# A two-model kernel: modulation sums off the tensor engine, one more early expert load, keys among the last transposes, outputs turned once per bank

## The chip, the cores and the metric

The kernel runs on one core of one Trainium2 chip. The metric is the device time of one execution in microseconds, as a median over runs; less is better. Everything is 32-bit floating point. A product in plain fp32 shows in the trace as two matmul entries; where three products of rounded parts take its place (`mm3`), each entry is one product of the fp32r type.

## What is computed

Two transformer blocks follow each other on the same 512 tokens of width 1024. Cut to what matters:

```python
# first block
m_lat = jnp.split((s_lat @ w_mod[l] + b_mod[l])[:, None, :], 6, axis=-1)
h_lat = modulate(rmsnorm(x_lat, norm1_g[l]), m_lat[0], m_lat[1])
mix_lat, mix_ctx = token_mixers(h_lat, h_ctx, w_in[l], ...)
x_lat = x_lat + m_lat[2] * (mix_lat @ w_out[l])
h_lat = modulate(rmsnorm(x_lat, norm2_g[l]), m_lat[3], m_lat[4])
x_lat = x_lat + m_lat[5] * expert_choice_ffn(h_lat, w_router[l], w_gate[l], w_up[l], w_down[l])
# second block
sh1, sc1, gt1, sh2, sc2, gt2 = jnp.split((jax.nn.silu(c) @ w_mod + b_mod)[:, None, :], 6, axis=-1)
x = x + gt1 * token_mixer(modulate_2(x, g, sh1, sc1), ...)
x = x + gt2 * conv_ffn(modulate_2(x, norm2_g[l], sh2, sc2), ...)
```

The six modulation vectors of a block are one 1024-vector times a 1024 by 6144 matrix. The experts are 16 gated networks of 24 MB each in all; each takes its 64 best tokens.

## The kernel before

The work is emitted by Python generators that are woven by weights (`weave`, `beside`); a scheduler then fixes each engine's order ahead of the run from these priorities and a model of times. On the chip every engine runs its own list in order, and a transfer is issued by the queue of the engine it stands on, nearly always SP's.

**Projections** (`g_proj`, L701 to 857, 52 to 222 us of the trace). Eleven blocks of 256 columns of `w_in` are loaded, split into a rounded part and a rest (`wsplit`, L1948 on: a copy on ScalarE, a subtraction on VectorE or GpSimd) and multiplied with the normed input. Results go through four PSUM banks. The block of values is written out from L789 on; convolution buffers `cr` and `cr2` are freed at the end.

**Modulation vectors** (`g_mods`, L652 on). Two half vectors of 512 columns make one vector. `mod_rows` (L510) loads a half vector's weights in four pieces of 512 KB into a ring of three buffers and multiplies eight k-steps, four of them in four column strips of the array; the two models' inputs stand as 32 weight columns. The row is copied out and then turned into the layout that is wanted: by transposes (`mod_cols`, L521), by products with the identity into a layout of 8 channels a partition (`mod_cols_pk`, L533), or spread over all partitions (`mod_bcast`, L545). Ten vectors are made this way beside the Fourier and the neighbourhood attention (`others`, L1464), while the delta rule (`g_dn`) is woven through.

**Experts** (`g_b`, L1617). Each expert has twelve loads of 2 MB: gate and up alternately, then down. They go into a ring of five buffers, later eight; `more` (L1633) lends rooms that are not used yet: expert 0's third load goes to the sum's room, its seventh to the inputs' room. The pair of experts gets its rows by an indirect transfer (`pair`, L1596) into `Y`, the same room that later takes the pair's output; the rows are transposed and scaled. The second model's context work (`g_c0`) is woven between and frees its room at its end; three more buffers then join the ring. `c_tile` (L2035) adds expert results to a tile of tokens, norms it, and at the last tile turns all four tiles in two halves (`to_hT2`, L1974) and splits them.

**Second mixer** (`part_c`). `c_att` begins with keys of two tiles at a time (`tok2`, L2004) and their rotation. `c_ssd` mixes values: for each pair of heads and each of four tiles of tokens, `mixed` (L2434) multiplies the weighted values, and adds the part `of` of the outer state by a product with the identity; both go to the same PSUM bank, which is scaled when its four tiles are done.

Of the kernel before, what the change touches and what calls it, by code (L numbers as in the profile page):

```python
# [390 lines left out]
class KA:  # L391
# [141 lines left out]
    def mod_cols_pk(self, s, wdram, bi, j, ring, rows, out):  # L533
        nc = self.nc
        t = self.big().rearrange("p (k g r) -> p k g r", k=8, g=4)
        for h in range(2):
            r = rows()
            self.mod_rows(s, wdram, 2 * j + h, ring, r)
            for kt in range(8):
                self.mm(t[64 * h:64 * h + 64, kt].rearrange("p g r -> p (g r)"), r[:, kt::8], self.ident)  # L540
        nc.vector.tensor_reduce(out, t[:, :, :, 0:2].rearrange("p c g r -> p c r g"), AX.X, OP.add)
        nc.vector.tensor_add(out, out, self.col("b_mod_pk", 8 * bi, 8)[:, :, None].to_broadcast([128, 8, 2]))
# [109 lines left out]
    def g_mods(self, tag, n):  # L652
        nc, I = self.nc, self.I
        self.md = tag
        with self.pool("mods") as P:
# [3 lines left out]
            self.mod_bcast(s1, wm, I["b_mod"], 2, wr, rows, self.gt1_b.ap(), self.sel)  # L659
            yield 0.1  # L660
            self.mod_cols_pk(s1, wm, 0, 3, wr, rows, mp[:, 0])
            yield 0.1
            self.mod_cols_pk(s1, wm, 1, 4, wr, rows, mp[:, 1])
            nc.vector.scalar_tensor_tensor(a2, mp[:, 1, :, 0], 1.0, self.col("norm2_g_pk", 0, 8), op0=OP.add, op1=OP.mult)
            yield 0.1
            self.mod_bcast(s1, wm, I["b_mod"], 5, wr, rows, self.gt2_b.ap(), self.sel)
            yield 0.1
            mc, a = self.m2c_b.ap(), self.ab2_b.ap()
            s2, wm = self.s2b.ap(), "w_mod_2"
            for i, j in enumerate((0, 1, 3, 4)):  # L670
                self.mod_cols(s2, wm, "b_mod_2", j, wr, rows, mc[:, i])
                yield 0.1
            for i, (m, r, n) in enumerate(((1, 0, "norm1_g_2"), (1, 1, "norm1_g_2"), (3, 0, "norm2_g_2"))):
                nc.vector.scalar_tensor_tensor(a[:, i], mc[:, m, :, r], 1.0, self.col(n, 0, 8), op0=OP.add, op1=OP.mult)
            for i, j in enumerate((2, 5)):
                for h in range(2):
                    r, g = rows(), rows()[0:1]
                    self.mod_rows(s2, wm, 2 * j + h, wr, r)
                    t = self.bank((128, 512), self.md)
                    self.mm(t, self.sel, r)  # L680
                    self.ld(g, I["b_mod_2"][0:1, 512 * (2 * j + h):512 * (2 * j + h) + 512], nc.scalar)
                    nc.vector.tensor_add(g, g, t[0:1])
                    nc.scalar.dma_start(self.gtd[i:i + 1, 512 * h:512 * h + 512], g)
                yield 0.1
# [16 lines left out]
    def g_proj(self, P):  # L701
# [91 lines left out]
        for t in range(4):  # L793
            z = nv()
            self.cp(z, self.tok(w, t))
            if t == 0:
                left()
            nc.scalar.dma_start(vdv[:, t], z)
        yield 0.04
        for t in range(2):  # L800
            self.cp(vc[:, t], self.tok(w, t, False))
        w.done()
# [4 lines left out]
        for i in range(2):  # L807
            nc.scalar.mul(q[:, i].rearrange("p (i r c) -> p r i c", i=4, r=8), self.chan(w, 128 * i).rearrange("p (r i c) -> p r i c", i=4, r=8), 0.125)
            yield 0.03
        w.done()  # L810
        w = block()
        for i in range(2):
            self.cp(k[:, i], self.chan(w, 128 * i), "v")
            if i == 0:
                next(gates)
                self.abT_b.free()
            self.cp(kc[:, i], self.chan(w, 128 * i, False))
            yield 0.05
# [6 lines left out]
        for a in range(2):  # L825
            w = block()
            for t in range(4):
# [4 lines left out]
                for e in range(2):  # L832
# [3 lines left out]
                    (nc.gpsimd.tensor_sub if e == 0 else nc.gpsimd.tensor_add)(o[:, :, :, e], o[:, :, :, e], u)  # L836
                yield 0.015
            if a == 1:
                for t in range(2):
                    self.cp(kc[:, t].rearrange("p m d -> p (m d)"), self.tok(w, t, False))  # L840
                yield 0.03
            w.done()
        w = block()
        for t in range(2):
            self.cp(v[:, t], self.tok(w, t, False))
        yield 0.03
        for t in range(4):
            self.cp(v[:, 2 + t], self.tok(w, t))
        yield 0.06
        w.done()  # L850
        w = block()
        for i in range(2):
            self.cp(self.uT_b.ap()[:, i], self.chan(w, 128 * i))
            yield 0.03
        w.done()
        cr.free()
        cr2.free()
# [648 lines left out]
class KB(KA):  # L1506
# [89 lines left out]
    def pair(self, pr, Y):  # L1596
        nc = self.nc
# [3 lines left out]
        nc.gpsimd.indirect_dma_start(Y, None, self.xnd, bass.IndirectOffsetOnAxis(self.ix[:, pr:pr + 1], 0))  # L1601
        yield
        for k4 in range(2):
            b = self.bank((128, 4, 128))
            for kk in range(4):
                nc.tensor.transpose(b[:, kk], Y[:, 4 * k4 + kk::8], self.ident)
# [10 lines left out]
    def g_b(self, experts=range(16)):  # L1617
# [15 lines left out]
        more = [None, None, sum_b.ap(), None, None, None, in_b.ap()]  # L1633
# [120 lines left out]
class Kern(KB):  # L1754
# [219 lines left out]
    def to_hT2(self, xs, half, a, b, tmp, bank=None):  # L1974
# [3 lines left out]
        for k in range(0, 8, n):  # L1978
# [5 lines left out]
            for kk in range(n):  # L1984
# [5 lines left out]
                (nc.gpsimd if kt % 2 else nc.vector).tensor_sub(lo, u, hi.bitcast(F32))  # L1990

# [12 lines left out]
    def tok2(self, w, t0, nt, tag="mm"):  # L2004
        n = w(0, 0).shape[1]
        b = self.bank((128, nt, n), tag)
# [28 lines left out]
    def c_tile(self, t, b):  # L2035
# [14 lines left out]
        c["r"].append(z(3))  # L2050
        if t == 3:
            mc, a = self.m2c_b.ap(), self.ab2_b.ap()
            for i in range(2):
                self.to_hT2([c["xn"][:, 2 * i], c["xn"][:, 2 * i + 1]], i, a[:, 0], mc[:, 0, :, 0], c["u"], lambda: self.bank((128, 2, 256)))
# [12 lines left out]
    def c_att(self, P):  # L2067
# [32 lines left out]
        for half in range(2):  # L2100
            for t in range(0, 4, 2):
                b = self.tok2(w, t, 2)
# [169 lines left out]
    def c_ssd(self, P):  # L2272
# [84 lines left out]
        for gr in range(4):  # L2357
# [76 lines left out]
            def mixed(k):  # L2434
                pr, c = k // 4, k % 4
                if c == 0:
                    ys[pr] = self.bank((128, 512), "y")
                yb, W, tk = ys[pr], Ws.pop(k), slice(128 * c, 128 * c + 128)
                for z in range(2):
                    for h in range(2):  # L2440
                        o = 128 * pr + 64 * h
                        self.mm(yb[64 * h:64 * h + 64, tk], (of if z else xs)[:, c, o:o + 64], self.ident if z else W[:, h], z == 0, z == 1)
# [338 lines left out]
```

## Time and profile before

| what | us |
|---|---|
| median of 3 runs (2982.39 to 2989.98) | 2982.91 |
| the profiled execution | 2982.76 |
| its span | 2980.9 |
| TensorE busy in the span | 2770.4 |
| VectorE | 1334.9 |
| ScalarE | 902.3 |
| GpSimd | 625.7 |

The span is what the profiler sees between the first and the last instruction; the rest of the profiled execution's time lies around it. A busy TensorE is one with matmuls in flight. Loading of weights is counted apart, since it runs beside the matmuls. The shares are means over stretches with different limits, so the rows below are taken by stretch. "Idle before" names what an engine waited for last.

### The profile page before, as it was taken

To read this page: it belongs to the slowest core of one execution; us is meant where nothing else is said; L and a number is where in the kernel's file an instruction comes from. 1 tells how busy PE (TensorE), PEld (TensorE's weight loads), DVE (VectorE), ACT (ScalarE), POOL (GpSimd) and SP (SyncE) were. 2 spreads that over 40 slices of the span, in tenths; PEclk is the share of its full clock that TensorE was granted. 3 is DMA by queue.
4 is the path that set the end of the run, shared out by engine and by line. 5 is a ranking of instruction groups with operands and counts; after the bars stand their busy time and mean duration, and the time that the engine had idled before them with its cause. 6 is when DMAs were issued, how large, how long until landed. Compare 5 with 4: busy or idle time off the path is not lost.

```text
span 2980.9 us, 41808 instructions
## 1 busy us (share of the span) xinstructions
PE 2770.4 (93%) x16824; PEld 1776.0 (60%) x16824; DVE 1334.9 (45%) x2654; ACT 902.3 (30%) x1836; POOL 625.7 (21%) x660
## 2 busy tenths in 40 slices
PE   7999989997999999988888789999999899999998
PEld 4894547765334333332222267777777688888886
DVE  5522445655121211111101167878787854454445
ACT  5511225532111010100000044545454543343333
POOL 3121224531000000000000024232323322332222
PEclk9999999998999999999999999999999999999999
DMA  6216661038999999989999923324242464242331
GB/s 268 75 34 200 209 218 32 30 121 309 397 430 430 429 429 430 429 371 430 431 431 430 387 88 105 118 64 123 72 120 74 134 232 160 94 154 95 97 99 57
DMA packets 213122, 658.53 MB, mean 221 GB/s; under 512 B 13816, under 2 KB 131192, under 8 KB 188352
## 3 DMA queue, kind: packets, MB, share of 16 engines
q1 hardware_dynamic: 185504, 601.73, 52.4%
q10 hardware_dynamic: 26272, 49.93, 4.7%
q0 software_dynamic: 1152, 4.19, 0.3%
q8 instruction: 133, 2.18, 0.3%
q14 instruction: 61, 0.50, 0.1%
HBM read 632.07 MB, written 23.73 MB: 220 GB/s over the span
## 4 chain that ended last, share of the span: by engine, by line
PE 68%; DMA 16%; DVE 10%; issue 2%; ACT 2%; POOL 2%; SPq 1%; ACTq 0%; POOLq 0%; DVEq 0%
PE bank_mm L399 29%; PE bigbank L399 20%; DMA l<-in_w_up 6%; PE bank_pj L399 6%; DMA l<-in_w_down 4%; PE bank_c L399 4%; PE bank_dn L399 2%; DMA mods<-in_cola 2%; DMA l<-in_w_gate 1%; PE bank_sm L399 1%; DVE base L2426 1%; DVE mix L2430 1%; PE bank_dnr L399 1%; DVE mix L2429 1%; PE bank_mm L2181 1%
## 5 line engine op out<-in xcount | busy, mean ns | idle before, releaser
L399 PE MATMUL bank_pj<-c,c 128*128 128x512 f32 (+2 forms) x1368 | 319.7, 376 | 0.3 <-DVE c L1964 0.3
L399 PE MATMUL bank_mm<-c,c 128*128 128x512 f32 (+1 forms) x1608 | 304.4, 347 | 4.9 <-ACT b L1987 3.2
L399 PEld LDWEIGHTS bank_mm<-c,c 128*128 128x128 f32 x1608 | 259.3, 191 | 44.2 <-ACT b L1987 3.6
L399 PE MATMUL bigbank<-l 128*64 128x512 f32 (+1 forms) x1104 | 266.1, 594 | 17.9 <-DMA l<-in_w_up 13.1
L399 PEld LDWEIGHTS bank_pj<-c,c 128*128 128x128 f32 (+1 forms) x1368 | 225.7, 189 | 50.7 <-issue 17.5
L1963 ACT CAST c<-base 128x1024 fp32r<-128x1024 f32 x147 | 152.8, 1045 | 254.3 <-PE bigbank L399 105.7
L1964 POOL TENSOR_TENSOR c<-base,c 128x1024 fp32r<-128x1024 f32 x47 | 116.7, 2483 | 472.9 <-ACT c L1963 404.6
L1964 DVE TENSOR_TENSOR c<-base,c 128x1024 fp32r<-128x1024 f32 x100 | 136.3, 1365 | 136.8 <-ACT c L1963 133.7
L399 PEld LDWEIGHTS bigbank<-l 128*64 128x64 f32 (+1 forms) x1104 | 80.9, 141 | 175.8 <-issue 140.4
L1692 DVE TENSOR_TENSOR b<-l,bigbank 128x512 f32<-128x512 f32 x32 | 20.5, 683 | 340.8 <-PE bigbank L399 293.5
L1691 ACT ACTIVATE l<-bigbank 128x512 f32<-128x512 f32 x32 | 17.4, 595 | 423.7 <-PE bigbank L399 423.7
L399 PE MATMUL bank_mm<-l 128*64 128x512 f32 (+2 forms) x528 | 124.8, 601 | 9.1 <-DMA l<-in_w_down 8.0
L399 PE MATMUL bigbank<-out,c 128*128 128x512 f32 x480 | 113.8, 397 | 1.9 <-ACT out L2524 1.8
L399 PE MATMUL bank_c<-b 128*128 128x256 f32 (+3 forms) x496 | 110.0, 373 | 1.9 <-ACT b L425 0.8
L399 PE MATMUL bank_mm<-h,sp 128*128 128x512 f32 (+3 forms) x544 | 105.5, 382 | 4.3 <-ACT h L644 3.8
L399 PEld LDWEIGHTS bank_dn<-dn 64*64 64x64 f32 x1920 | 74.8, 134 | 55.0 <-issue 39.3
L399 PEld LDWEIGHTS bigbank<-out,c 128*128 128x128 f32 x480 | 91.7, 192 | 23.0 <-ACT out L2524 2.2
L399 PE MATMUL bigbank<-b,l 128*64 128x512 f32 x352 | 84.9, 614 | 21.8 <-DMA b<-in_w_up 10.9
L1717 DVE TENSOR_TENSOR b<-bank_mm,ab 64x512 f32<-64x512 f32 x16 | 10.9, 683 | 208.1 <-PE bank_mm L399 208.1
L1786 ACT ACTIVATE b<-bank_c,base 128x256 f32<-128x256 f32 x20 | 11.3, 563 | 304.6 <-PE bank_c L399 304.6
L399 PEld LDWEIGHTS bank_c<-b 128*128 128x128 f32 (+1 forms) x496 | 80.4, 188 | 37.2 <-issue 23.9
L399 PE MATMUL bigbank<-c,ffn 128*128 128x512 f32 x432 | 100.3, 390 | 0.0
(538 smaller groups left out, 5060.7 us busy)
## 6 DMA issues: line engine op xcount, KB each, us to landing
l<-in_w_up SPq DMA_DIRECT2D x36, 2048.0 KB, 14.6
l<-in_w_down SPq DMA_DIRECT2D x31, 2048.0 KB, 17.0
l<-in_w_gate SPq DMA_DIRECT2D x29, 2048.0 KB, 18.2
mods<-in_cola SPq DMA_DIRECT2D x80, 512.0 KB, 4.9
base<-in_w_in SPq DMA_DIRECT2D x68, 512.0 KB, 3.7
b<-in_w_gate SPq DMA_DIRECT2D x15, 2048.0 KB, 34.0
base<-in_w_gate SPq DMA_DIRECT2D x13, 2048.0 KB, 16.9
wo<-in_w_up SPq DMA_DIRECT2D x13, 2048.0 KB, 33.8
```

Of the source, the lines that this page charges most:

```text
L399: self.mm_ins = self.nc.tensor.matmul(out, l, r, start=start, stop=stop).ins
L1691: nc.scalar.activation(s, ac[0][:, j], AF.Silu)
L1692: nc.vector.tensor_mul(hid[:, 512 * j:512 * j + 512], s, ac[1][:, j])
L1717: nc.vector.tensor_mul(Y[pp, 0:512], dn[0:64], gt2[0:64, 0:512])
L1786: nc.scalar.activation(y, b, AF.Identity, scale=wc(1), bias=self.col(bname, i))
L1963: nc.scalar.copy(hi, raw)
L1964: (nc.vector if self.wn % 4 in self.losplit else nc.gpsimd).tensor_sub(lo, raw, hi.bitcast(F32))
L2181: nc.tensor.transpose(tb[:, z], p[:, 128 * (g0 + z):128 * (g0 + z) + 128], self.ident)
L2426: nc.vector.scalar_tensor_tensor(E[:, h], rw[:, h, 0], gc(1, 0, h), E[:, h], op0=OP.subtract, op1=OP.min)
L2429: nc.vector.tensor_scalar(W[:, h], cb[:, c, 0], gc(0, 0, h), None, op0=OP.mult)
L2430: nc.vector.scalar_tensor_tensor(W[:, h], cb[:, c, 1], gc(0, 1, h), W[:, h], op0=OP.mult, op1=OP.add)
```

## The change

- Four of the ten modulation vectors (two of each model) leave `g_mods`. A new generator, `g_late_mods`, makes them in `g_proj`, a step at a time between the projections from the block of values on: weights come in pieces of 256 KB, VectorE and ScalarE scale them by the input's entries, VectorE and GpSimd add them up, and a few matmuls with a column of ones close each half vector. `cr` and `cr2` are freed earlier for this.
- Expert 0's eighth load goes to the outputs' room (`out_b`). Every pair's rows are now fetched into the room of the first gate vector (`gt1_b`), not into `Y`.
- The turning of the tiles becomes a generator. The first half is turned at the third tile; at the fourth, keys of the first two tiles are computed between the groups of the second half, one tile at the start and one before the last group, and copied to SBUF, from where `c_att` takes them.
- `mixed` turns the four tiles of `of` with four transposes into the bank first and adds the weighted values on top; the products with the identity go.

```diff
+    def mod_sums(self, s, wdram, j, rings):
+        nc, (wr, da, pa, pp) = self.nc, rings
+        wv = self.block(wdram, j)
+        d, o = da(), pa()
+        for kt in range(8):
+            w, c = wr(), s[:, kt, 0:1]
+            self.ld(w, wv[:, kt])
+            if kt == 0:
+                nc.vector.tensor_scalar(d, w, c, None, op0=OP.mult)
+            elif kt in (1, 3, 6):
+                z = o if kt == 1 else pp()
+                nc.scalar.activation(z, w, AF.Copy, scale=c)
+                if kt > 1:
+                    nc.gpsimd.tensor_add(o, o, z)
+            else:
+                nc.vector.scalar_tensor_tensor(d, w, c, d, op0=OP.mult, op1=OP.add)
+            if kt == 3:
+                yield
+        nc.gpsimd.tensor_add(o, o, d)
+        self.msum = o
+
+    def mod_close(self, o, h, bias, out, pk):
+        p, n = (slice(64 * h, 64 * h + 64), slice(0, 8)) if pk else (slice(0, 128), slice(4 * h, 4 * h + 4))
+        t = self.bank((128, 8), "md")
+        for c in range(8 if pk else 4):
+            self.mm(t[p, n.start + c:n.start + c + 1], o[:, c::8] if pk else o[:, c * 128:(c + 1) * 128], self.km("one", 1))
+        self.nc.vector.tensor_add(out[p, n], t[p, n], bias[p, n])
+
+    def g_late_mods(self, P):
...
+        of = [Ring(P, [512], 2, more=[Buf(self.M, [512]) for _ in range(2)])] + [Ring(self.M, [512], n) for n in (1, 2, 1)]
+        owed = []
...
+            for h in range(2):
+                yield from self.mod_sums(s, w, 2 * j + h, of)
+                if owed:
+                    owed.pop()()
+                owed.append(lambda o=self.msum, h=h, n=n, name=name, out=out, pk=pk: self.mod_close(o, h, self.col(name, n, 8), out, pk))
+                yield
...
     def g_proj(self, P):
...
             if t == 0:
                 left()
+                cr.free()
+                cr2.free()
+                sums = self.g_late_mods(P)
+            if t % 2 == 0:
+                next(sums)
...
     def pair(self, pr, Y):
-        nc.gpsimd.indirect_dma_start(Y, None, self.xnd, bass.IndirectOffsetOnAxis(self.ix[:, pr:pr + 1], 0))
+        nc.gpsimd.indirect_dma_start(G, None, self.xnd, bass.IndirectOffsetOnAxis(self.ix[:, pr:pr + 1], 0))
...
-        more = [None, None, sum_b.ap(), None, None, None, in_b.ap()]
+        more = [None, None, sum_b.ap(), None, None, None, in_b.ap(), out_b.ap()]
...
+        if t == 2:
+            for _ in turned(0):
+                pass
         if t == 3:
+            last, kb = turned(1), self.bank((128, 2, 256), "c0")
             for i in range(2):
-                self.to_hT2([c["xn"][:, 2 * i], c["xn"][:, 2 * i + 1]], i, a[:, 0], mc[:, 0, :, 0], c["u"], lambda: self.bank((128, 2, 256)))
+                self.tok2(self.pre[0], i, 1, b=kb[:, i:i + 1])
+                for _ in range(3 if i == 0 else 1):
+                    next(last)
+            for _ in last:
+                pass
+            self.cp(self.rr.rearrange("p (t n) -> p t n", t=2), kb, "a")
...
-                b = self.tok2(w, t, 2)
+                b = self.rr.rearrange("p (t n) -> p t n", t=2) if half + t == 0 else self.tok2(w, t, 2)
...
                 if c == 0:
-                    ys[pr] = self.bank((128, 512), "y")
+                    b = ys[pr] = self.bank((128, 512), "y")
+                    for z in range(4):
+                        nc.tensor.matmul(b[:, 128 * z:128 * z + 128], of[:, z, 128 * pr:128 * pr + 128], self.ident, start=z == 0, stop=False, is_transpose=True)
-                for z in range(2):
-                    for h in range(2):
-                        o = 128 * pr + 64 * h
-                        self.mm(yb[64 * h:64 * h + 64, tk], (of if z else xs)[:, c, o:o + 64], self.ident if z else W[:, h], z == 0, z == 1)
+                for h in range(2):
+                    o = 128 * pr + 64 * h
+                    self.mm(yb[64 * h:64 * h + 64, tk], xs[:, c, o:o + 64], W[:, h], False, c == 3)
```

## Rows read from the trace of the kernel before

**Rows 1.** Busy time by stretch: PE, PEld, DVE, ACT, POOL; granted clock; DMA share, GB/s.
```profile
122.00:222.00 100.00, 100.00 (x821) 93.75 (x820) 25.09 (x78) 20.76 (x36) 21.70 (x27) 1.00 0.12 42
222.00:452.00 230.00, 212.34 (x2081) 112.33 (x2080) 92.48 (x222) 55.93 (x171) 49.51 (x82) 1.00 0.64 206
...
740.00:750.00 10.00, 8.70 (x32) 3.80 (x34) 1.55 (x4) 3.00 (x5) 0.00 (x0) 0.65 0.22 72
750.00:1290.00 540.00, 523.75 (x2257) 209.97 (x2254) 97.34 (x188) 58.08 (x121) 24.56 (x24) 1.00 1.00 426
1290.00:1297.00 7.00, 5.92 (x16) 1.31 (x14) 0.76 (x2) 1.17 (x2) 4.08 (x4) 1.00 0.10 37
...
1724.00:1733.00 9.00, 4.10 (x21) 2.35 (x19) 6.58 (x17) 7.23 (x15) 3.89 (x6) 0.83 0.14 59
1733.00:1740.00 7.00, 3.71 (x14) 2.57 (x14) 6.57 (x17) 5.78 (x11) 3.56 (x5) 0.73 0.18 75
...
1740.00:2380.00 640.00, 606.44 (x4049) 483.68 (x4050) 510.86 (x1162) 307.68 (x708) 190.16 (x211) 0.98 0.33 97
...
2180.00:2200.00 20.00, 16.25 (x145) 13.43 (x146) 19.31 (x56) 12.85 (x35) 4.83 (x7) 1.00 0.45 131
```

**Rows 2.** Groups by form, 222 to 452: count, busy, mean ns, idle before and releasers.
```profile
L399 PE MATMUL bank_mm<-mods,ab 128*32 128x512 f32 x320 | 71.5, 603 | 11.7 <-DMA mods<-in_cola 11.2 <-DVE dn L427 0.3 <-ACT dn L425 0.2
...
L399 PE MATMUL bigbank<-base,mods 128*64 128x128 f32 x64 | 8.7, 288 | 0.0
...
L528 PE MATMUL bank_mm<-base,mods 128*128 128x128 f32 x32 | 5.2, 285 | 0.0
```

**Rows 3.** Groups by form: the delta rule's products, 222 to 452, then 452 to 645.
```profile
L399 PE MATMUL bank_dn<-dn 64*64 64x64 f32 x880 | 45.8, 226 | 2.3 <-DVE dn L1014 0.6 <-DVE base L1190 0.6 <-ACT dn L1006 0.5
...
L399 PE MATMUL bank_dn<-dn 64*64 64x64 f32 x1008 | 49.2, 225 | 1.9 <-DVE dn L427 1.3 <-DVE dn L1014 0.6
```

**Rows 4.** Groups by form, 122 to 222: products with few columns; one vector operation.
```profile
L399 PE MATMUL bank_mm<-base,l 128*64 128x4 f32 x96 | 3.0, 199 | 0.0
...
L399 PE MATMUL bank_mm<-l,a 128*128 128x24 f32 x8 | 1.0, 258 | 0.0
L742 DVE SCALAR_TENSOR_TENSOR l<-l 128x512 f32<-128x512 f32 x1 | 0.7, 693 | 5.8 <-ACT l L741 5.8
```

**Rows 5.** Groups by form, 452 to 700: additions of 512 columns on GpSimd.
```profile
L1385 POOL TENSOR_TENSOR l<-l 128x512 f32<-128x512 f32 x8 | 11.6, 1446 | 33.7 <-DVE l L1384 33.7
```

**Rows 6.** In order of time (start, us): a split's end; a block's last copy out.
```profile
174.92 2.41 POOL L1964 TENSOR_TENSOR sp<-base,sp 128x1024 fp32r<-128x1024 f32 x1 [2.52 <-ACT sp L1963]
...
191.81 0.42 DVE L427 COPY l<-bank_mm 128x256 f32<-128x256 f32 x1
```

**Rows 7.** TensorE's waits, 743 to 1297: us in total, times, longest.
```profile
PE bigbank L399 <- DMA l<-in_w_up: 1.3, 1, 1.3
```

**Rows 8.** The waits of SP's queue, 1255 to 1300.
```profile
SPq L430 <- PE bank_c L1878: 16.1, 1, 16.1
```

**Rows 9.** The chain that ended last, 700 to 800: the gather of rows.
```profile
730.58 10.59 DMA b<-xnorm,ab
```

**Rows 10.** In order of time, TensorE: the first keys.
```profile
1740.01 7.51 PE L399 MATMUL bank_mm<-c,c 128*128 128x256 f32 x48 [3.19 <-ACT b L1987]
```

**Rows 11.** Busy time of entries on the mixing bank alone, by stretch: PE, PEld, DVE.
```profile
1740.00:2380.00 640.00, 40.47 (x512) 31.10 (x512) 10.88 (x16) 0.98 0.33 97
```

**Rows 12.** Groups by form, 1740 to 2380: transposes of 128 by 128.
```profile
L2181 PE MATMUL bank_mm<-base,mix 128*128 128x128 f32 x288 | 44.5, 282 | 6.1 <-DVE mix L2171 5.4 <-ACT mix L425 0.4 <-DVE mix L427 0.2
```

**Rows 13.** In order of time: casts on VectorE, then a subtraction on GpSimd.
```profile
1736.21 0.28 DVE L1989 CAST c<-b 128x256 fp32r<-128x256 f32 x1
1736.63 0.80 DVE L1989 CAST c<-b 128x256 fp32r<-128x256 f32 x1 [0.15 <-ACT b L1987]
...
1736.56 0.72 POOL L1990 TENSOR_TENSOR c<-b,c 128x256 fp32r<-128x256 f32 x1 [0.56 <-DVE c L1989]
```

**Rows 14.** All instructions on the modulation tiles: their loads' time to landing.
```profile
DMA to landing us min/median/max: 3.8/4.9/9.7
```

More of the change, by code (lines that the diff above doesn't have):

```diff
@@ L801, in g_proj @@
             self.cp(vc[:, t], self.tok(w, t, False))
+        next(sums)
         w.done()
@@ L808, in g_proj @@
             nc.scalar.mul(q[:, i].rearrange("p (i r c) -> p r i c", i=4, r=8), self.chan(w, 128 * i).rearrange("p (r i c) -> p r i c", i=4, r=8), 0.125)
+            next(sums)
             yield 0.03
@@ L816, in g_proj @@
                 self.abT_b.free()
+                next(sums)
             self.cp(kc[:, i], self.chan(w, 128 * i, False))
+            next(sums)
             yield 0.05
@@ L836, in g_proj @@
                     (nc.gpsimd.tensor_sub if e == 0 else nc.gpsimd.tensor_add)(o[:, :, :, e], o[:, :, :, e], u)
+                if t % 2 == 0:
+                    next(sums)
                 yield 0.015
@@ L840, in g_proj @@
                     self.cp(kc[:, t].rearrange("p m d -> p (m d)"), self.tok(w, t, False))
+                next(sums)
                 yield 0.03
@@ L845, in g_proj @@
             self.cp(v[:, t], self.tok(w, t, False))
+        next(sums)
         yield 0.03
@@ L848, in g_proj @@
             self.cp(v[:, 2 + t], self.tok(w, t))
+            if t == 1:
+                next(sums)
         yield 0.06
@@ L853, in g_proj @@
             self.cp(self.uT_b.ap()[:, i], self.chan(w, 128 * i))
+            if i == 0:
+                next(sums)
             yield 0.03
         w.done()
-        cr.free()
-        cr2.free()
+        for _ in sums:
+            pass
     def a_gates(self):
@@ L1971, in mm3, with to_hT2, g_hT2 @@
             self.mm(out, L[a], R[b], first and i == 0, last and i == 2)
-    def to_hT2(self, xs, half, a, b, tmp, bank=None):
+    def to_hT2(self, *args):
+        for _ in self.g_hT2(*args):
+            pass
+    def g_hT2(self, xs, half, a, b, tmp, bank=None):
         nc = self.nc
@@ L2002, in chan2, with tok2 @@
         return b
-    def tok2(self, w, t0, nt, tag="mm"):
+    def tok2(self, w, t0, nt, tag="mm", b=None):
         n = w(0, 0).shape[1]
-        b = self.bank((128, nt, n), tag)
+        b = self.bank((128, nt, n), tag) if b is None else b
         for t in range(nt):
```

47 lines of the change are left out of this document (22 added, 25 removed).

## The prediction

> **What bounds the kernel now.** I read the stretches first, then inside each the groups by form, the waits, the order of time and last the chain. The table by stretch [rows 1] gives four places the change touches. In 122 to 222 us (the second half of the first model's projections) TensorE is busy 100.00 of 100 us; nothing put on it there is free. In 222 to 452 us (Fourier, neighbourhood attention, delta rule, modulation vectors woven together) it is busy 212.3 of 230. From 750 to 1290 us (experts with the second model's context work between them) TensorE has 523.75 of 540 and the DMA share is 1.00: two limits at once. From 1740 to 2380 us (second mixer) TensorE has 606 of 640, VectorE 511; in a slice among the mixing matmuls (2180 to 2200) VectorE has 19.3 of 20 and TensorE 16.3, so VectorE ends last there. The profiled execution took 2982.76 us, its span 2980.9; the runs' median is 2982.91, so the sum is made against 2982.8. About 0.3% (9 us) is what a measurement can tell from no change.
>
> **Part 1, modulation sums, removed.** Of the 20 half vectors (rows of 512 columns) in 222 to 452 us, 8 leave. A row's eight k-steps are 16 matmul entries; 320 entries hold TensorE for 71.5 us [rows 2], so 3.58 us a row, 28.6 us for eight. All four rows in the packed layout leave, and with them their 64 turning entries, 8.7 us; so do 4 of the 8 rows turned by transposes, half of 5.2 us, 2.6 us [rows 2]. Together 39.9 us. The stretch's wait for these loads, 11.2 us [rows 2], could shrink by 8/20, 4.5 us; I take nothing, since the three buffers of the ring and the two rows emitted at a time stay.
>
> Is something else late once that is gone? 212.3 - 39.9 is 172.4 us of work; with the idle 17.7 us as it is, 190 us. VectorE's 92, ScalarE's 56 and GpSimd's 50 us [rows 1] are no limit. The delta rule is a serial recurrence: its 64-column matmuls come at 880 in 230 us, 3.8 a us, would come at 4.6, and in 452 to 645 us they do come at 1008 in 193 us, 5.2 a us [rows 3]. So I take -39.9. Bounds: -44.4 with the wait, and -25 if the waits on small steps grow to fill 15 us (17.7 us idle nearly doubled).
>
> **Part 1, added.** TensorE gets 48 closing matmuls with one moving column: 32 with 64 weight columns, 16 with 128. The nearest rows are the gate sums: 96 entries (48 matmuls, 64 weight columns, 4 moving) in 3.0 us, 0.0625 each, and 8 entries (4 matmuls, 128 columns, 24 moving) in 1.0 us, 0.25 each [rows 4]. 32 by 0.0625 plus 16 by 0.25 is 6.0 us, all on the path because TensorE is full there; half to double, 3 to 12 us, as ends.
>
> Eight rows also bring 64 loads of 256 KB on SP's queue, 40 vector operations (at most 0.69 us each [rows 4], 28 us), 24 scalings on ScalarE (priced alike, 17 us) and 24 additions on GpSimd (1.45 us [rows 5], 35 us). The three engines have 25, 21 and 22 us of 100 busy there [rows 1]. The cover is depth: the weight split finished at 177.3 us feeds a block that starts after the last copy of the block before it, 191.8 us [rows 6], 14 us later; and the DMA share is 0.12. What waits behind a late load: the vector instruction that reads it holds VectorE's queue, behind it copies out of PSUM, and behind these, after four banks, TensorE. SP's queue is passed too: a load whose ring buffer is not yet read holds the next projection weights. I take 0 for this; ends -0 and +10 (a gain is excluded, since work is only added). The closing product of a row is emitted two steps later, so its wait for GpSimd's last addition should be over. Part 1: -39.9 + 6.0 = -33.9.
>
> **Part 2, the early expert load.** The eighth load of expert 0 goes to the outputs' room; before, it waited for a buffer that TensorE had to read. It moves 2.1 MB, 4.9 us at the expert stretch's 426 GB/s, into 740 to 750 us, where the DMA share is 0.22 [rows 1]. I do not take 4.9. In 750 to 1290 TensorE is busy 97%, and of its idle time only three short waits were for expert loads, the largest 1.3 us [rows 7]; at most 3.9 us can come back. And the lead is given up at 1290 to 1297 us, DMA share 0.10 [rows 1]: SP stood 16.1 us for the context work to leave its room [rows 8], and that end is TensorE's. Against it: the gather of rows that opens the expert stage took 10.6 us beside loads [rows 9], now with one more load behind it; 0 to +4.9 us if it waits for that load whole. The gathers now all land in the first gate vector's room; pair 1's gather must wait on GpSimd's queue for pair 0's transposes, but GpSimd has nothing to do behind it (0.00 of 740 to 750). The final norm's load into the same room, on ScalarE's queue, waits for transposes of an expert earlier, long done. I take 0, ends -3.9 and +4.9. The Trainium skill's page "DMA: Bandwidth & Descriptors" (Queues, rings and completion order) says that each DMA engine takes turns between queues packet by packet; by that the gather would lose its turn only, nearer 0 than +4.9. The gather's 10.6 us for half a megabyte shows that its turns were few.
>
> **Part 3, keys between the last transposes.** At 1740.0 us, 48 matmuls of keys for two tiles start and take 7.5 us [rows 10], after the last transposes. Before them TensorE has 4.1 of 9 and 3.7 of 7 us busy [rows 1], 8.2 us free. The first tile's 24 need only the first half of the turned input. What ends last instead: copying the second half out, 7 us from the last norm on, on ScalarE, VectorE and GpSimd (5.8, 6.6, 3.6 of 7 us busy); and the first half's turning now stands ahead of the last tile's squares, which may come 1 to 2 us later. So -7.5 + 1.5 = -6; ends -7.5 and +2. The copy of the two tiles' keys to SBUF and the later rotation from there lie beside full TensorE time.
>
> **Part 4, output turned once.** All entries into the mixing bank hold TensorE 40.5 us [rows 11]. Half of them, the identity products, go: -20.2. 64 transposes come: 288 of a like form hold 44.5 us [rows 12], 0.155 each, 9.9 us. That is -10.3 us of TensorE, in slices where VectorE ends last [rows 1]. I take 3 of it; ends -10.3 and +2 (all four tiles must be ready before the first product).
>
> **Sum.** -33.9 + 0 - 6 - 3 = -42.9; 2982.8 - 42.9 = 2939.9, predicted 2940 us.
>
> **Rivals.** (a) The emptied stretch fills with waits: the recurrence and the loads then set its pace, half of the 39.9 us comes, 2940 + 20 = 2960. For it: 17.7 us are idle already. Against it: the 5.2 a us [rows 3]. (b) VectorE and GpSimd hold each other up in the projections: a cast that took 0.28 us took 0.80 when it fell on a GpSimd subtraction of 0.72 us [rows 13]. If the two never ran together there, 25 + 28 and 22 + 35 make 110 us in a stretch of 100: 10 us more, 2950. The Trainium skill's "GPSIMD Engine Reference" (8. Key points) says that GpSimd shares its SBUF interfaces with VectorE, in contention above all where VectorE has two SBUF inputs, as most of the added operations do; by that (b) would hold for nearly all of them. (c) The other side: the loads are not covered. Each of the 16 steps takes four loads through a ring of four; if each step exposes one landing, 4.9 us in the median [rows 14], the projections grow by 78 us, 3018. It decides from 3.3 us a step on (43 + 9 over 16). Against it: 14 us of lead [rows 6] and a DMA share of 0.12. (d) The keys or the early load don't move: the order on TensorE stays, 2946; or the load comes through whole, 2935.
>
> **Chances.** Forecast with (d) 0.70 (2925 to 2951), (a) 0.15, (b) 0.08, (c) 0.05, 0.02 for a change of order elsewhere that eats the gain. Bounds of the parts: part 1 from -44 + 3 to -25 + 12, the others from -22 to +9 when all fall alike, which they won't. The range 2920 to 2968 takes in (a) and (b) and leaves out (c) and the tails. Faster by over 0.3%: 0.91; within: 0.04; slower: 0.05.
>
> **What would show it.** Part 1: the stretch from the end of projections to the end of the modulation vectors falls from 230 to about 190 us, and the projections keep TensorE above 98% and grow by 6. Wrong if TensorE's idle time there passes 30 us, or if the projections show waits for splits. Part 2: the eighth load is issued with the seventh, yet the DMA gap before the last context work is as long or longer. Part 3: 24 of the key matmuls start before the last tile's norm; the first product of the next block starts some 6 us sooner after the last transposes. Part 4: the mixing bank's time falls from 40 to 30 us, the stretch by less.

## The result and the profile after

The changed kernel takes 2954.76 us (median of 4 runs, 2953.37 to 2956.10), 0.9896 of the kernel before (95% interval 0.9879 to 0.9913; the median before is 2985.20 with a fourth run), some 30 us less. Its profiled execution took 2954.31 us against 2982.76 before: 28.5 us less, where the prediction had 42.9. The time lies inside the predicted range, 15 us above the forecast. The profiled executions let the 28.5 be placed. For that the run is cut at seven events that every kernel here has. They are read from the traces in order of time: the last product of the first model's projections (end), the last product on modulation rows (end), the first gather of rows, the first product of the norm that closes the first model, the first product into the bank of the second mixer's channel blocks, VectorE's last read of the mixing bank, and the end. The view is the busy time by stretch of the kernel after, with the columns of [rows 1]; the stretches are those between the events.

```profile
52.00:236.10 184.10, 180.54 (x1252) 160.35 (x1251) 117.56 (x202) 79.60 (x118) 74.36 (x55) 0.98 0.42 139
236.10:419.20 183.10, 178.74 (x1843) 98.00 (x1844) 85.15 (x202) 51.54 (x164) 49.34 (x84) 1.00 0.52 166
419.20:701.70 282.50, 263.57 (x2971) 194.64 (x2969) 173.37 (x421) 132.38 (x356) 110.14 (x177) 0.98 0.31 115
701.70:1683.40 981.70, 883.28 (x3779) 328.17 (x3780) 148.09 (x274) 81.74 (x166) 33.08 (x33) 0.99 0.99 418
1683.40:1712.80 29.40, 22.03 (x101) 14.30 (x99) 21.34 (x43) 18.59 (x33) 13.74 (x16) 0.94 0.34 116
1712.80:2335.50 622.70, 589.38 (x3751) 464.97 (x3751) 508.60 (x1152) 302.40 (x696) 189.24 (x210) 0.98 0.32 95
2335.50:2952.50 617.00, 596.35 (x2676) 492.13 (x2676) 294.44 (x349) 225.46 (x280) 179.85 (x98) 0.98 0.38 127
```

The same cuts of every trace give these lengths (us). They are the table that the rest argues from:

| kernel | projections | vectors, delta rule | to the gather | experts | last transposes | second mixer | rest |
|---|---|---|---|---|---|---|---|
| before | 167.2 | 233.5 | 277.9 | 980.6 | 36.2 | 617.4 | 616.2 |
| after | 184.1 | 183.2 | 282.4 | 981.7 | 29.4 | 622.7 | 617.0 |
| e5, after again | 188.1 | 185.2 | 279.8 | 980.9 | 29.9 | 621.9 | 617.8 |
| e1, part 1 alone | 183.5 | 183.0 | 282.7 | 981.1 | 37.8 | 614.9 | 616.6 |
| e2, part 3 alone | 169.0 | 235.6 | 275.7 | 980.1 | 31.5 | 620.6 | 614.5 |
| e3, part 4 alone | 169.0 | 233.1 | 278.0 | 981.4 | 37.2 | 617.1 | 614.2 |
| e4, after without part 4 | 185.5 | 187.1 | 282.8 | 979.5 | 30.6 | 618.6 | 614.7 |
| e6, adjacent columns | 184.9 | 185.1 | 282.3 | 980.4 | 32.3 | 621.0 | 616.9 |
| e7, after, VectorE relieved | 186.2 | 186.5 | 282.4 | 982.2 | 30.7 | 604.8 | 615.6 |
| e8, e4 and relieved | 186.2 | 183.3 | 282.2 | 983.0 | 29.2 | 605.9 | 618.0 |
| e9, e1 and relieved | 184.6 | 183.7 | 282.7 | 981.6 | 37.2 | 608.4 | 616.8 |
| e10, last addition on VectorE | 183.6 | 183.9 | 279.7 | 981.0 | 32.3 | 619.9 | 617.6 |
| e11, short closings, relieved | 185.3 | 183.8 | 280.2 | 982.2 | 30.7 | 604.9 | 615.1 |

Read down, equal kernels differ by 1 to 4 us in a stretch, so means are used. The ten traces with part 1 have 185.2 us of projections against 168.4 in the three without (+16.8), 184.5 against 234.1 in the vectors' stretch (-49.6) and 281.7 against 277.2 to the gather (+4.5). Part 1 is worth 28.3 us. The experts take 981.4 with part 2 and 981.0 without it. The last transposes take 30.7 with part 3 and 37.1 without, and what follows in the second mixer is not the same in all.

**Projections.** Groups of the kernel after, two on TensorE by form (122 to 245 us) and two on VectorE (122 to 240 us); then, in order of time, one subtraction on GpSimd and the VectorE operation beside it:

```profile
L399 PE MATMUL bank_md<-base,l 128*64 128x1 f32 x64 | 8.3, 259 | 0.0
L399 PE MATMUL bank_md<-base,l 128*128 128x1 f32 x32 | 3.8, 240 | 0.0
```
```profile
L548 DVE SCALAR_TENSOR_TENSOR l<-l,ab 128x512 f32<-128x512 f32 x16 | 16.3, 1016 | 10.8 <-DMA l<-in_cola 10.7
L541 DVE TENSOR_SCALAR l<-l,ab 128x512 f32<-128x512 f32 x8 | 8.3, 1037 | 17.1 <-POOL l L551 14.0 <-DMA l<-in_cola 3.1
```
```profile
153.85 2.39 POOL L2013 TENSOR_TENSOR sp<-base,sp 128x1024 fp32r<-128x1024 f32 x1
...
153.92 2.59 DVE L541 TENSOR_SCALAR l<-l,ab 128x512 f32<-128x512 f32 x1 [1.47 <-POOL l L551]
```

The closing products take 12.1 us, not 6.0 [rows 4]: 0.130 an entry with 64 columns of weights, where the gate sums with as many had 0.031. VectorE's products take 1.0 us in the mean against the 0.693 of [rows 4], because some that begin while a GpSimd operation runs end only behind it: 2.59 us next to a subtraction of 2.39, in a group where the median is 0.49.

**Vectors and delta rule.** Groups by form, 236 to 419 us: the row products of [rows 2] are 192 entries for 12 rows, and their wait for loads is 2.5 us where it was 11.2.

```profile
L399 PE MATMUL bank_mm<-mods,ab 128*32 128x512 f32 x192 | 46.6, 604 | 2.6 <-DMA mods<-in_cola 2.5
L399 PE MATMUL bank_dn<-dn 64*64 64x64 f32 x798 | 37.5, 224 | 0.7 <-DVE dn L1063 0.6 <-ACT dn L425 0.2
```

The second row has 798 of the delta rule's entries where [rows 3] had 880: 82 of them now come in the next stretch. The same two stretches of the kernel before, for the sums below:

```profile
219.20:452.70 233.50, 215.84 (x2150) 115.07 (x2152) 93.58 (x223) 57.22 (x175) 52.90 (x88) 1.00 0.64 205
452.70:730.60 277.90, 260.90 (x2864) 191.57 (x2864) 170.54 (x415) 129.98 (x349) 108.14 (x174) 0.97 0.32 116
```

**Experts.** SP's queue in order of time, its wait at the end of the first model's context work, and the stretch where the lead is given up (compare [rows 8] and the row of 1290 to 1297 in [rows 1]):

```profile
700.51 0.33 SPq L430 DMA_DIRECT2D l<-in_w_gate  x1
700.89 0.43 SPq L430 DMA_DIRECT2D b<-in_w_up  x1
```
```profile
SPq L430 <- PE bank_c L1927: 16.1, 1, 16.1
```
```profile
1261.00:1268.00 7.00, 5.92 (x16) 1.31 (x14) 0.75 (x2) 1.17 (x2) 4.09 (x4) 1.00 0.10 39
```

The eighth load goes out 0.4 us behind the seventh, where it was 19.3 us behind it (729.41 and 748.72 in the trace of before), and all of that is gone where SP waits the same 16.1 us.

**Last transposes.** TensorE in order of time: keys go between the transposes from 1699.0 us on, and the next block's first product follows the last of them at 1712.8.

```profile
1698.99 0.84 PE L399 MATMUL bank_c<-c,c 128*128 128x256 f32 x5
...
1705.92 3.05 PE L399 MATMUL bank_c<-c,c 128*128 128x256 f32 x17
...
1712.84 11.19 PE L399 MATMUL bank_pj<-c,c 128*64 128x512 f32 x48 [1.25 <-ACT b L2040]
```

**Second mixer.** The mixing bank's entries alone by stretch, TensorE's waits for that bank (two rows of the kernel before, then two of the kernel after), and two stretches of the slices in which it is filled:

```profile
1712.80:2335.50 622.70, 33.89 (x320) 22.58 (x320) 10.15 (x15) 0.98 0.32 95
```
```profile
PE bank_y L399 <- POOL mix L2431: 2.6, 5, 0.9
...
PE bank_y L399 <- DVE mix L2399: 2.4, 1, 2.4
```
```profile
PE bank_y L399 <- POOL mix L2496: 12.8, 6, 4.0
PE bank_y L2504 <- DVE base L2514: 4.3, 3, 3.0
```
```profile
1990.00:1998.00 8.00, 5.37 (x27) 3.80 (x27) 6.28 (x18) 2.80 (x8) 1.79 (x2) 0.57 0.47 146
1980.00:1990.00 10.00, 8.63 (x81) 7.46 (x79) 9.68 (x24) 5.11 (x12) 5.00 (x5) 1.00 0.19 56
```

The bank's busy time falls from 40.5 [rows 11] to 33.9 us. The waits for it grow from 5 to 17 us: for the weights, which GpSimd multiplies last, and for VectorE to leave the bank. In the pieces around, TensorE is busy 14.0 of 18 us, and its clock stands at 1.2 GHz for most of eight.

### The profile page after: what moved, and what is told of

It reads as the page before. It is cut to its first block, busy times and chain, and to the rows that moved or that the text cites. A ratio compares the mean times of both kernels' runs of the same rounds, so it can differ in the third digit from the quotient of the medians.

```text
span 2952.5 us, 41373 instructions
## 1 busy us (share of the span) xinstructions
PE 2746.8 (93%) x16520; PEld 1768.5 (60%) x16520; DVE 1373.7 (47%) x2687; ACT 918.0 (31%) x1858; POOL 662.9 (22%) x684
## 5 line engine op out<-in xcount | busy, mean ns | idle before, releaser
L399 PE MATMUL bank_pj<-c,c 128*128 128x512 f32 (+2 forms) x1368 | 326.0, 380 | 1.2 <-ACT b L2040 1.2
L399 PE MATMUL bank_mm<-c,c 128*128 128x512 f32 (+1 forms) x1560 | 297.3, 349 | 1.3 <-DVE c L2013 1.3
L399 PEld LDWEIGHTS bank_mm<-c,c 128*128 128x128 f32 x1560 | 253.1, 190 | 39.6 <-DVE c L2013 1.7
L399 PE MATMUL bank_mm<-l 128*64 128x512 f32 (+2 forms) x528 | 126.8, 605 | 10.3 <-DMA l<-in_w_down 8.1
L399 PEld LDWEIGHTS bank_c<-b 128*128 128x128 f32 (+1 forms) x496 | 80.4, 188 | 37.2 <-issue 23.9
L399 PEld LDWEIGHTS bank_mm<-h,sp 128*128 128x128 f32 (+1 forms) x544 | 86.6, 188 | 24.4 <-ACT h L681 4.0
```

What stands on the lines that cost most here:

```text
L399: self.mm_ins = self.nc.tensor.matmul(out, l, r, start=start, stop=stop).ins
```

## The experiments

Eleven runs, each timed four to twelve times beside the kernel before. Their intervals reach 3 to 5 us to either side, so two of them can be told apart in the medians from some 6 us on; below that the stretches of the table, one trace each, have to decide.

**e1 to e4: the parts apart.** e1 is before with part 1, e2 with part 3, e3 with part 4; e4 is after without part 4, as

```diff
-                for h in range(2):
-                    o = 128 * pr + 64 * h
-                    self.mm(yb[64 * h:64 * h + 64, tk], xs[:, c, o:o + 64], W[:, h], False, c == 3)
+                for z in range(2):
+                    for h in range(2):
+                        o = 128 * pr + 64 * h
+                        self.mm(yb[64 * h:64 * h + 64, tk], (of if z else xs)[:, c, o:o + 64], self.ident if z else W[:, h], z == 0, z == 1)
```

> The kernel before with part 1 alone (four of the modulation vectors' sums beside the projections). The traces of before and after stand 28.9 us apart at the row gathers that open the expert stage, and only part 1 lies ahead of them. Theory A (the steps add): 28.9 us less than before, 0.990 of it; in its trace the projections end 17 to 18 us later than before (closing products about 12 us instead of the 6 of the prediction, and about 5 us of lower granted clock near 134 and 144 us), and the stretch behind them is 46 us shorter. Rival B (the prediction's own sizes, with the difference lost behind): 34 us less. Rival C (the lower clock near 134 to 148 us is chance, not a consequence of the part): the projections end only 12 us later here and the gain is 33 us or more.

Measured: 2955.19 us, 0.9915 of before (0.9902 to 0.9928). The three stretches of part 1, columns as above:

```profile
52.00:235.50 183.50, 180.32 (x1252) 160.29 (x1251) 117.27 (x202) 79.30 (x118) 73.50 (x55) 0.98 0.44 140
235.50:418.50 183.00, 178.63 (x1844) 98.05 (x1844) 85.13 (x202) 51.53 (x164) 49.32 (x84) 1.00 0.55 166
418.50:701.20 282.70, 264.17 (x2971) 195.07 (x2969) 173.29 (x422) 132.52 (x356) 110.12 (x176) 0.98 0.32 116
```

The same places and sizes as in after: A holds, and part 1 alone gives nearly all that the change gives. Of C one half stands: the projections of e2 and e3, without part 1, have a granted clock of 0.99 where before had 1.00, so a little of it comes and goes. But with part 1 it is 0.96 to 0.98 in all ten traces. 185 us by 0.02 to 0.04, less 169 by 0 to 0.01, is an estimate of about 4 us more (2 to 7 by the ends), and TensorE was busy all but 3.2 of the 183.5 us here.

> The kernel before with part 3 alone (key products between the last transposes). Theory A: the first product of the next block starts 6 to 7 us sooner and the lead is kept to the end, so 6 us less than before. Rival B (the 4.6 us that the kernel after gives back inside the second mixer are part 3's: the keys' copy through SBUF and the other alternation of copies between ScalarE and VectorE make VectorE late): the lead is there at 1750 us and gone by 2330 us, 1 to 2 us less than before.

Measured: 2985.07 us, 1.0006 (0.9996 to 1.0016). Its last transposes and second mixer:

```profile
1712.50:1744.00 31.50, 23.23 (x101) 14.99 (x99) 22.74 (x47) 19.64 (x36) 14.33 (x17) 0.89 0.32 108
1744.00:2364.70 620.70, 591.07 (x3922) 467.53 (x3922) 504.00 (x1149) 300.43 (x692) 189.77 (x209) 0.99 0.33 95
```

The lead is there (31.5 against 36.2 us) and the mixer takes back 3.2 of it (620.6 against 617.4): B. By one trace that is no more than equal kernels differ by, but e4 and e1, with part 3 and without it, differ alike (618.6 against 614.9). No gain is left that the runs can tell.

> The kernel before with part 4 alone (output turned once into the mixing bank). Theory A (part 4 gives back what is lost in the second mixer): TensorE's busy time on the mixing bank falls from 59 to 35 us, its waits for GpSimd's weights grow from 3 to about 13 us and those for the bank from 2 to 4, the granted clock falls in more slices, and the end comes 3 to 5 us later than before. Rival B (the prediction): 3 us less than before. Rival C: no difference, within 1 us, since VectorE ends last there either way.

Measured: 2983.71 us, 1.0006 (0.9997 to 1.0015); the mixer takes 617.1 us, as before. The mixing bank's groups by form:

```profile
L399 PE MATMUL bank_y<-mix,mix 128*64 128x128 f32 x256 | 24.4, 295 | 3.2 <-POOL mix L2431 3.2
L2439 PE MATMUL bank_y<-base,mix 128*128 128x128 f32 x64 | 11.1, 292 | 4.7 <-DVE base L2449 4.7
```

The same groups in the trace of the kernel before:

```profile
L399 PE MATMUL bank_y<-mix,mix 128*64 128x128 f32 x256 | 30.2, 290 | 2.6 <-POOL mix L2431 2.6
L399 PE MATMUL bank_y<-base,mix 128*64 128x128 f32 x256 | 28.9, 285 | 2.5 <-DVE mix L2399 2.4
```

C: the busy time of the rows falls from 59 to 35.5 us, waits grow a little, and the end doesn't move. The growth of the waits to 13 us that A expected needs part 3 as well.

> The kernel after without part 4. Theory A: 4 to 5 us faster than the kernel after, 33 us less than before, with the lead of about 34 us at the first mixer output still there at the last. Rival B (the loss inside the second mixer is part 3's): 3 us slower than the kernel after, some 26 us less than before. Rival C (part 4 does nothing): the same as after, 28 to 30 us less than before, and the lead is lost between the first and the last mixer output here too.

Measured: 2951.14 us, 0.9891 (0.9877 to 0.9906), with this mixer:

```profile
1717.50:2336.10 618.60, 587.76 (x3922) 465.47 (x3922) 504.70 (x1152) 301.12 (x694) 191.32 (x210) 0.99 0.33 95
```

3.6 us below after, 4 us shorter in the mixer: the direction of A, but not settled by these runs, as the intervals overlap.

**e5, after again; e7 and e8, VectorE relieved.** e7 is after, e8 is e4, each with one scaling of the mixing weights moved:

```diff
+                for h in range(2):
+                    nc.scalar.activation(W[:, h], cb[:, c, 0], AF.Copy, scale=gc(0, 0, h))
                 nc.scalar.activation(E, E, AF.Exp)
                 for h in range(2):
-                    nc.vector.tensor_scalar(W[:, h], cb[:, c, 0], gc(0, 0, h), None, op0=OP.mult)
```

> The kernel after, unchanged, beside the next three on one chip, and a second trace of its second mixer. From the first product of the second mixer's next block to its last mixed output the trace of after took 622.7 us, 5 us more than before and 4 us more than without part 4, with the granted clock lowered in five places there against two to four. Theory A (part 4 costs through these lowered stretches, and they come back in every execution): over 620 us again, the clock lowered in at least four places. Rival B (where the clock falls there is chance): 614 to 618 us, and the median within 2 us of the kernel without part 4.

Measured: 2957.40 us, 0.9911 (0.9897 to 0.9924). The mixer took 621.9 us with the clock lowered in four places, so what after lost there comes back: A. The mixers of e6 and e10 below are the same and took 621.0 and 619.9 us, with the clock lowered in four and three places.

> The kernel after, and the first scaling of each mixing weight (128 scalings of 128 columns, 48 us of VectorE in the second mixer) goes to ScalarE. Theory A (VectorE sets the pace in the mixing slices, so part 4's 24 us less of TensorE there became waits): the waits of TensorE for the weights fall from 13 us to under 5, the mixer is 10 us shorter or more. Rival B (the chain ScalarE, VectorE, GpSimd of a weight sets it, however the work is divided): the waits stay above 10 us, the end moves by less than 3 us. Rival C: ScalarE becomes late, slower by 3 us or more.

Measured: 2942.13 us, 0.9852 (0.9837 to 0.9867), 15 us below e5. Its mixer by stretch, and TensorE's wait for the weights:

```profile
1720.00:2324.80 604.80, 581.87 (x3755) 458.17 (x3755) 472.40 (x1024) 336.29 (x821) 184.61 (x210) 1.00 0.34 96
```
```profile
PE bank_y L399 <- POOL mix L2497: 2.6, 5, 0.9
```

A: VectorE goes from 508.6 us in after to 472.4, the waits for the weights from 12.8 to 2.6, the mixer from 622 to 605, and the clock stays at 2.4 GHz all through. Of the 17.9 us between the mixers of after and e7, 10.4 are idle time of TensorE and 7.5 busy time of the same products, so the clock has a share in this gain; no run separates it from the waits.

> The kernel after without part 4, with the same scalings on ScalarE. Theory A: TensorE's 24 us of identity products come onto the path once VectorE is relieved, so this gains less than the same edit with part 4 does: 3 to 6 us less than without it, and 5 us or more slower than the kernel with part 4 and the edit. Rival B: the same gain or none in both, so part 4 is worth nothing either way.

Measured: 2939.69 us, 0.9840 (0.9825 to 0.9856); mixer 605.9 us against 604.8 in e7. B: with VectorE out of the way too, part 4 is worth 1 us in the mixer and nothing in the whole.

**e9: the same relief without parts 2 to 4** (e1 and the diff above).

> The kernel before with part 1, and the first scaling of the mixing weights on ScalarE; parts 2, 3 and 4 are not in it. Theory A (part 3's lead at the last transposes is real and is given back in the second mixer because VectorE sets the pace there): with VectorE relieved, part 3 is worth its whole 6 us, so this is 6 us slower than the run without part 4 and with the same scalings, some 2946 where that took 2939.7; against part 1 alone the scalings gain 8 us or more. Rival B (the lead of part 3 is lost for another reason, or is only the lower clock of the emptied stretch): 0 to 3 us slower than that run.

Measured: 2949.81 us, 0.9896 (0.9878 to 0.9913). Last transposes and mixer:

```profile
1684.60:1721.80 37.20, 23.92 (x101) 16.54 (x100) 24.30 (x52) 19.68 (x35) 15.66 (x18) 0.77 0.31 103
1721.80:2330.20 608.40, 586.28 (x3928) 465.53 (x3926) 476.74 (x1013) 335.98 (x819) 186.00 (x207) 1.00 0.33 95
```

The same two stretches in e8:

```profile
1686.70:1715.90 29.20, 22.12 (x102) 13.73 (x100) 21.34 (x43) 18.47 (x33) 13.73 (x16) 0.94 0.34 117
1715.90:2321.70 605.80, 584.88 (x3927) 464.91 (x3927) 475.94 (x1023) 338.84 (x823) 185.03 (x210) 1.00 0.34 96
```

A: 10 us above e8. Both stretches together take 645.6 us here and 635.1 in e8, so part 3 is worth 10.5 us once VectorE is relieved; without the relief it was 652.7 (e1) against 649.2 (e4) and 653.6 (before) against 652.1 (e2). The relief alone (e1 to e9) gives 5.4 us by the medians, whose intervals overlap, and 6.5 us of mixer; 8 were expected. Of rival B's second half, the lower clock, little stands: the last transposes take 32.3 us in both e6 and e10 at a mean clock of 0.79, with part 3, and 37.2 us in e3 and e9 at 0.77, without it, so about 5 us of the lead don't come from the clock.

**e6, e10, e11: the price of the closings.** e6 and e10 are after with one line each (in e6 the values of the packed vectors come out in another order, so it serves for its times alone):

```diff
-            self.mm(t[p, n.start + c:n.start + c + 1], o[:, c::8] if pk else o[:, c * 128:(c + 1) * 128], self.km("one", 1))
+            self.mm(t[p, n.start + c:n.start + c + 1], o[:, 64 * c:64 * c + 64] if pk else o[:, c * 128:(c + 1) * 128], self.km("one", 1))
...
-        nc.gpsimd.tensor_add(o, o, d)
+        nc.vector.tensor_add(o, o, d)
```

> The kernel after with one edit: the closing products of the packed sums take 64 adjacent columns as their weights instead of every eighth; the columns so come out in another order, so four of the vectors' values stand in the wrong places. In the trace of after 64 entries with strided weights of 64 columns took 8.3 us (0.130 each), where the gate sums with adjacent weights of 64 columns took 0.031 each. Theory A (the stride makes the weight load long): the 64 entries fall to 2 us, the end comes 6 us sooner. Rival B (a fresh weight tile of any kind costs 0.13 us): nothing changes, within 1 us.

Measured: 2955.85 us, 0.9897 (0.9882 to 0.9912), with this group:

```profile
L399 PE MATMUL bank_md<-base,l 128*64 128x1 f32 x64 | 4.6, 201 | 3.5 <-POOL l L551 3.5
```

Half of A: the stride made the load of the weights long (8.3 to 4.6 us), though not by all that the gate sums promised; the other 2.6 us above their price stay open. TensorE then waits 3.5 us for GpSimd's additions, and the projections end no sooner (184.9, with TensorE busy 177.0 of it where after had 180.5 of 184.1).

> The kernel after, and the last of a row's additions (the two partial sums) on VectorE instead of GpSimd. In the trace of after VectorE's first product of the next row waited 14.0 us in all for that addition. Theory A (TensorE covers all that): the projections end at the same place within 2 us, no change. Theory B (the clock falls in the projections because VectorE, GpSimd and the transfers work at once): the lowered stretches there go or stay, which the trace shows. Rival C (VectorE, now at 64 of 100 us, becomes late): the projections grow by 3 us or more.

Measured: 2952.96 us, 0.9902 (0.9887 to 0.9917). VectorE's first product of a row (duration in ns, min, median and max, then first and last start):

```profile
L541 DVE TENSOR_SCALAR l<-l,ab x8: 481/486/577, 131.7 to 210.6; 128x512 f32<-128x512 f32 x8
```

A: 183.6 us, with the 14.0 us of VectorE's wait gone, and no product of this line held beyond 0.58 us (2.61 in after). The lower clock stays (0.97), so B's mechanism isn't shown by this.

e11 is e8 with that last addition, and

```diff
+            w = w.rearrange("p (r c) -> p c r", c=8) if pk else v(w)
...
-        for c in range(8 if pk else 4):
-            self.mm(t[p, n.start + c:n.start + c + 1], o[:, c::8] if pk else o[:, c * 128:(c + 1) * 128], self.km("one", 1))
+        for c in range(8):
+            q, m = (p, c) if pk else (slice(64 * (c % 2), 64 * (c % 2) + 64), n.start + c // 2)
+            self.mm(t[q, m:m + 1], o[:, 64 * c:64 * c + 64], self.km("one", 1))
```

> The kernel after without part 4, the scalings of the mixing weights on ScalarE, and the closing products in 64 pieces of 64 adjacent columns (the packed rows' sums are laid out in that order by the way their inputs are read), with the last addition on VectorE. Theory A (what the closings cost is the load of their weights, and the waits for GpSimd that took the gain of adjacent columns go with its last addition): 64 pieces by 0.072 make 4.6 instead of 12.1 us, so the projections end 7 us sooner and the whole takes 7 us less than the same kernel without the short closings (2939.7), some 2933. Rival B (the sums themselves end too late, whoever adds last): TensorE waits for them 4 us or more, within 3 us of that kernel. Rival C (reading inputs at a stride slows VectorE and ScalarE): their operations on these rows take 20% longer or more and the projections end later.

Measured: 2936.37 us, 0.9844 (0.9826 to 0.9862), the lowest median of all, but not told apart from e8. Three groups by form of its projections:

```profile
L399 PE MATMUL bank_md<-base,l 128*64 128x1 f32 x128 | 6.9, 199 | 2.8 <-DVE l L554 2.8
```
```profile
L551 DVE SCALAR_TENSOR_TENSOR l<-l,ab 128x512 f32<-128x512 f32 x16 | 22.2, 1388 | 7.7 <-DMA l<-in_cola 7.6
L547 ACT ACTIVATE l<-l,ab 128x512 f32<-128x512 f32 x8 | 7.9, 992 | 16.3 <-DMA l<-in_cola 16.3
```

B, with C's slower operations but not its later end: the closings fall from 12.1 to 6.9 us, but VectorE's products take 1388 ns in the mean (1016 in after, 1117 in e10, which has the last addition on VectorE too) and ScalarE's 992 (720), with half of the rows read at a stride. TensorE waits 5.6 us for VectorE in all, and the projections take 185.3 us as in the others.

## Why the prediction was right in sign and 15 us short in size

The time lies inside the range, but outside the forecast's own case (2925 to 2951 us). The range reaches to it only because it was drawn to take in rivals (a) and (b), and neither came at its price, so this is luck in part. Term by term:

| term | forecast | shown |
|---|---|---|
| part 1, removed | -39.9 | -45.1 (-49.6, +4.5 behind it) |
| part 1, added | +6.0 | +16.8 |
| part 2 | 0 | +0.4 |
| part 3 | -6 | between -1.5 and -3.5 |
| part 4 | -3 | 0 alone, +1 to +4 in the mixer beside part 3 |
| sum | -42.9 | -28.5 (the profiled executions) |

**Part 1, removed: near in the sum, by two misses that offset each other.** In the vectors' stretch and the one behind it TensorE's busy time fell by 34.4 us, not 39.9: the twelve rows that stay hold it for 46.6 us, so the eight that left were worth 24.9 and not 28.6. Its idle time fell by 11.4 us, where the prediction took nothing; 8.7 of them are the waits for loads (11.2 to 2.5), priced at 4.5 and then left out. In the vectors' stretch alone idle time fell from 17.7 to 4.4 us. The stretch takes 183 us against the 190 forecast, and 4.5 us come back behind it with the 82 delta-rule entries that are now done later. Rival (a) is out: the emptied stretch did not fill with waits. So is (c): the projections waited 1.6 us for what the sums brought, not 78.

**Part 1, added: mis-sized, and the row of failure is [rows 4].** Three pieces make the 16.8 us. The closing products took 12.1 instead of 6.0, at the upper end of the bounds, and all of that excess is in the packed ones (8.3 instead of 2.0). The nearest row had weights in adjacent columns; these stood every eighth, and e6 shows that this was 3.7 us of it. About 4 us are the lower granted clock (estimated at e1), a piece that the prediction did not have. The waits (1.6 us) were in the +10 that it kept as an end. "The cover is depth" held only because the closings were dear: e6 and e11 make them shorter by 3.7 and 5.2 us and get waits in their place (TensorE idle 7.9 and 7.5 us, 3.6 in after), so the additions on the other engines end hardly sooner than the products that hid them. The projections stayed at 98% busy, as said, which was no proof of cover.

**Rival (b) had the mechanism and not the price.** VectorE's 40 operations took 39.7 us instead of 28, since it and GpSimd do hold each other up. The prediction set beside this what the Trainium skill's "GPSIMD Engine Reference" (8. Key points) says of shared SBUF interfaces, and took from it the case of two inputs; VectorE's 2-port modes stand there too. The trace agrees for operations that begin beside one of GpSimd's (2.59 us beside 2.39 with one input; 2.85 against a median of 0.76 with two), but by the median (0.75 us) most of the products were not held up, so (b) did not hold for nearly all of them. TensorE saw 1.6 us of it.

**Part 2: right.** The load came sooner and the lead was given up at the same wait. The gather that stands beside it kept TensorE waiting 13.6 us instead of 12.0: 1.6 us more, not the 4.9 of waiting for that load whole. That agrees with queues taking turns, as the Trainium skill's "DMA: Bandwidth & Descriptors" (Queues, rings and completion order) has it.

**Part 3: right in its own place, wrong that this is the end of it.** The last transposes took 6.4 us less, against 6 forecast, with the last tile's norm 3.2 us late (its normalizing step starts 24.5 us sooner than before, those of the first two tiles 27.7) where 1 to 2 were expected. The step that failed is the sentence that the copy and the later rotation "lie beside full TensorE time": the prediction read VectorE at its limit in a slice of the mixer for part 4 and did not ask it of part 3. What the runs show in its place: without the relief 1.5 to 3.5 us of the lead are left at the last mixed output, and e8 against e9, where VectorE's work in the mixer is 29 and 25 us less than in e4 and e1, shows it whole. That VectorE's late end is what takes the lead is the reading that fits both; only this one relief was tried.

**Part 4: the row was read rightly and then not believed.** The text says that VectorE ends last there and still takes 3 of 10.3 us. The work did fall, by 6.6 us, and the waits grew by 12. Whether part 4 costs some 3 us beside part 3 stays open by the intervals of the medians, though all four mixers with both parts (619.9 to 622.7 us) are longer than e4's 618.6; that it gains nothing is shown three times (e3, e4, e8). The lower clock goes with it but isn't shown to be its cause: in after the mixer's TensorE is idle 33 us at a mean clock of 0.98, in e7 to e9 it is idle 21 to 23 us at 1.00, and in e1 29 us, also at 1.00.

## What to carry to other kernels

A stretch where one engine is full can be emptied onto others, and the gain is then what the next engine in line leaves of it: before counting a lead or a saving, read which engine ends last in every stretch that follows, not only in the one that is edited. The best step here was none of the four parts but a relief of that engine: 128 small scalings on ScalarE gave 11 us beside parts 1 to 3 (15 with part 4 too; 5 beside part 1 alone, within the intervals) and made part 3's lead worth its price. Price a small product by a row whose weights are laid out in memory as its own are.

## What the runs showed of the hardware

- Weights of 64 columns read at every eighth column took 0.130 us an entry and 0.072 with adjacent columns. VectorE and ScalarE pay for such a stride too: with half of the rows read so, the means went from 1117 (e10) to 1388 and from 720 to 992 ns, and in the trace of e11 an operation on a strided row takes about 1.2 and 1.3 us where one on an adjacent row takes 0.75 and 0.72.
- Rows summed by form can fall more than the engine does: the mixing bank's groups fell by 24 us and their busy time in the stretch by 6.6, since the entries overlap.
- The granted clock fell to 1.2 GHz in the projections while TensorE was busy (in after at 134 and 144 us, with TensorE busy without a break from 116 to 140), in all ten traces where VectorE, GpSimd and the transfers were made busier beside it (mean clock 0.96 to 0.98), and hardly in the other three (0.99 to 1.00). Why is open; e10, with less on GpSimd and more on VectorE, didn't change it.
